# The down projections of a two-layer decoder trunk: two matmuls in place of three per weight block

## The chip, the cores and the metric

The kernel runs on one core of a Trainium2 chip. The metric is the device time of one execution in microseconds (us). Five engines work side by side, each through a queue of its own in order: TensorE multiplies (PE in the profile; PEld is its loading of weights), VectorE (DVE) and ScalarE (ACT) do elementwise work, GpSimd (POOL) does a little of it too, and SyncE (SP) issues transfers. TensorE writes its products into PSUM, which has eight banks of 512 float32 columns on 128 partitions.

## The reference, cut to what matters

The trunk has two layers, 256 tokens and a width of 1024. Layer 0 has a recurrent mixer, layer 1 sparse attention; after each comes a squared-ReLU MLP with 4096 hidden units. The part that the change touches is the second product of the MLP:

```
def _sq_relu_mlp(h, w_up, w_down):
    u = jax.nn.relu(h @ w_up)
    return (u * u) @ w_down
...
        h = _rmsnorm(x, norm_ffn[i])
        x = x + _sq_relu_mlp(h, mlp_w_up[i], mlp_w_down[i])
    return _rmsnorm(x, norm_final)
```

Everything is float32. `w_down` is 4096 by 1024 for each layer.

## The kernel before, in words

Everything is kept transposed: features on the 128 partitions, the 256 tokens along the free dimension. The residual stream `xt` is eight chunks of 128 features by 256 tokens.

To come near float32 with TensorE's rounded float32 format (`fp32r`), each operand is held as two parts, a rounded one (`h`) and the rest (`l`). A product of two operands is then three matmuls, which `mm3` (lines 373 to 377) issues for every 128 by 128 block of weights: rounded weights times rounded activations (line 375), rounded weights times the rest of the activations (line 376), and the rest of the weights times rounded activations (line 377). All three add into the same 256 columns of a bank, and each has its own load of 128 by 128 weights. The fourth product, rest times rest, is left out. The 256 tokens are read in the order 0, 128, 1, 129 and so on (`turn`), so that neighbouring columns of the bank hold tokens 128 apart (`pairs`); whoever reads the bank puts them back (`nat`).

Weights come from memory in pieces of 128 by 1024 (512 KB), in one fixed order. SP loads a piece into one of five `raw` tiles, ACT rounds it into one of seven `hi` tiles (line 322), and DVE subtracts to make one of seven `lo` tiles (line 331). In the MLPs this is driven by `tick` (line 344), called once for each piece that TensorE takes: it issues the subtraction for one piece, whatever was put off, and the rounding of the next, as long as fewer than six pieces (`LOOK`) are ahead of the one taken. The first layer's mixer and the attention have their order of work worked out by a planner beforehand (`Section`); the MLPs between them are written in program order, and each engine works through its own part of that order.

`mlp` (line 827) has two stages. The up stage makes 32 chunks of hidden units, 24 matmuls each; DVE and ACT square them and leave both parts of a chunk side by side in one tile, `uhl[i]`, rounded part in the first 256 columns, the rest in the other 256. The down stage has eight columns of output (`m`), of 32 blocks each: four pieces of weights, eight blocks to a piece, 96 matmuls in all. A column has one bank to itself, out of a ring of six. At its end DVE adds the bank to the residual (`residual`, line 589), and `epilogue(m)` starts the next norm: ACT scales the chunk, POOL squares it and adds it to a running sum. After the MLP of layer 0 this is `to_mix` (line 870), which also has DVE make the rest of the scaled chunk one `tick` later; after that of layer 1 it is `to_final` (line 1378), and there the column `m = 7` has a little more work between its third and fourth piece: four one-column matmuls (`late`, line 582) that sum the squares of the first seven chunks.

```
            for m in range(8):
                z = next(zrot)[:, :S]
...
                    wh, wl = get("dn%d" % layer, m * 4 + j)
                    for k in range(8):
                        w, i = slice(k * P, (k + 1) * P), j * 8 + k
                        mm3(z, wh[:, w], wl[:, w], uh[i], ul[i], i == 0, i == NF - 1)
                    if j == 3:
                        residual(z, m)
                        epilogue(m)
                    tick()
```

Of the kernel before, what the change touches and what calls it, by code (L numbers as in the profile page):

```python
# [12 lines left out]
F32 = mybir.dt.float32  # L13
F32R = mybir.dt.float32r
AF = mybir.ActivationFunctionType
OP = mybir.AluOpType
# [3 lines left out]
P = 128  # L20
S = 256
D = 1024
KC = D // P
NF = 32
# [248 lines left out]
def trunk_kernel(ctx: ExitStack, tc: tile.TileContext, x_in, vec_in, const_in, w2_in, wts, out):  # L273
    nc = tc.nc
    ctx.enter_context(tc.manual_schedule())
    pe, dve, act, pool = nc.tensor, nc.vector, nc.scalar, nc.gpsimd
# [9 lines left out]
    def bank(i):  # L286
        return psum.tile([P, 512], F32, name="bank%d" % i, tag="bank%d" % i)

    def rotation(*ids):
        while True:  # L290
            for i in ids:
                yield bank(i)
# [43 lines left out]
    def later(fn):  # L336
        deferred.append(fn)

    def flush():
        todo, deferred[:] = deferred[:], []  # L340
        for fn in todo:
            fn()

    def tick(lo=None, hi=None, n=1):
        for i in range(max(n, 1)):
            more = n and state["split"] - state["get"] < LOOK
            if more:
                split_lo(lo)
            if i == 0:
                flush()  # L350
            if more:
                split_hi(hi)

    def get(name, idx):
        i = state["get"]
        assert order[i] == (name, idx), (order[i], name, idx)
        state["get"] += 1
        assert state["lo"] > i
        return hi_t[i % NSPL], lo_t[i % NSPL]

    def turn(x):
        return x.rearrange("p (a b) -> p b a", a=2)

    def pairs(z):
        return z.rearrange("p (b a) -> p b a", a=2)

    def nat(z):
        return z.rearrange("p (b a) -> p a b", a=2)

    def two(x):  # L370
        return x.rearrange("p (a b) -> p a b", a=2)

    def mm3(ps, wh, wl, xh, xl, start, stop):
        ps, xh, xl = pairs(ps), turn(xh), turn(xl)
        pe.matmul(ps, wh, xh, start=start, stop=False)  # L375
        pe.matmul(ps, wh, xl, start=False, stop=False)  # L376
        pe.matmul(ps, wl, xh, start=False, stop=stop)  # L377

    def diff(o, a, h):
        return lambda e: e.tensor_tensor(o, a, h.bitcast(F32), op=OP.subtract)  # L380
# [10 lines left out]
    class Section:  # L391
# [86 lines left out]
        def proj(self, name, idx, b, t, step, xs=None, xk=None):  # L478
            wh, wl, wk = self.weight(name, idx, t)
            z = self.bank((name, idx), b, zcols)  # L480
            xs, xk = xs or [(hh[:, k], hl[:, k]) for k in range(KC)], xk or hkey
            for i in range(4):
                def run(e, i=i):
                    for k in (2 * i, 2 * i + 1):
                        w = slice(k * P, (k + 1) * P)
                        mm3(z(), wh[:, w], wl[:, w], xs[k][0], xs[k][1], k == 0, k == KC - 1)
                self.add("pe", 0.7 if self.carried else 0.68, run, r=wk + list(xk[2 * i:2 * i + 2]), w=[("ps", b)], t=t + i * step)
            return z, ("ps", b)
# [49 lines left out]
    xt = xpool.tile([P, KC, S], F32, name="xt")  # L538
# [50 lines left out]
    def residual(z, m):  # L589
        dve.tensor_tensor(two(xt[:, m]), two(xt[:, m]), nat(z), op=OP.add)  # L590


    with ExitStack() as ph:
# [41 lines left out]
        for k in range(KC):  # L635
# [6 lines left out]
                w=[("hh", k)], t=t)  # L642
# [3 lines left out]
        for q in range(4):  # L646
            for i in range(NFINE):
                w = slice(256 * q, 256 * q + 256)
# [6 lines left out]
        for a, b, n in ((0, 2, 2), (0, 1, 1), (4, 6, 2), (4, 5, 1), (0, 4, 1)):  # L655
            add("dve", 0.07 + 0.267 * n, lambda e, a=a, b=b, n=n: e.tensor_tensor(
                x2[:, a:a + n], x2[:, a:a + n], x2[:, b:b + n], op=OP.add), r=[("x2", b + i) for i in range(n)],
                w=[("x2", a + i) for i in range(n)], t=4 + a / 4)
# [44 lines left out]
        def nextbank():  # L703
            zb["n"] += 1
            return (0, 1, 2, 3, 4, 5, 7)[(zb["n"] - 1) % 7]

        def conv(m, t):
            b = nextbank()
            if m < NFINE:
                wh, wl, _ = sec.weight("in", 8 + m, t)  # L710
                z, zk = sec.bank(("in", 8 + m), b, zcols), ("ps", b)
                for k in range(KC):
                    def run(e, k=k):
                        w = slice(k * P, (k + 1) * P)
                        mm3(z(), wh[:, w], wl[:, w], hh[:, k], hl[:, k], k == 0, k == KC - 1)
                    add("pe", 0.323, run, r=[("hi0", m, k // 2), ("lo0", m, k // 2), ("hi", m), ("lo", m), hkey[k]],
                        w=[zk], t=m * 0.33 + k * NI * PJ / 2 if m < NI else t + k * PJ / 2)
            else:
                z, zk = sec.proj("in", 8 + m, b, t, PJ)
            t += 4 * PJ  # L720
            x, xk = xps[m % 3], ("xp", m % 3)
            bk = ("xb", m)
            add("dve", 0.34, lambda e: e.tensor_tensor(two(x[:, 3:]), nat(z()), two(rs), op=OP.mult), r=[zk, "rs"], w=[xk], t=t)
            add("act", 0.49, lambda e: e.activation(xb[m], x[:, 3:], AF.Identity, bias=col(V_CB, m), scale=cw(3, m)),
                r=[xk], w=[bk], t=t)
            for i in range(3):
                add("dve", 0.4, lambda e, i=i: e.scalar_tensor_tensor(xb[m], x[:, i:i + S], cw(i, m), xb[m], op0=OP.mult,
                                                                      op1=OP.add), r=[xk], w=[bk], t=t)
# [82 lines left out]
        for m in range(8):  # L811
            wh, wl, wk = sec.weight("out", m, to + 2.65 * m)
            b = nextbank()
            z = sec.bank(("out", m), b, zcols)
# [12 lines left out]
    def mlp(layer, epilogue, first, late=None):  # L827
        with ExitStack() as ph:
            up = ph.enter_context(tc.tile_pool(name="up%d" % layer, bufs=1, side="right"))
            tmp = ph.enter_context(tc.tile_pool(name="mtmp%d" % layer, bufs=2))  # L830
            uhl = [up.tile([P, 2 * S], F32R, name="uhl", tag="uhl", bufs=NF) for _ in range(NF)]
            uh, ul = [x[:, :S] for x in uhl], [x[:, S:] for x in uhl]
            zrot = rotation(*((LEADS[layer] + i) % 6 for i in range(6)))

            def up_post(m, z):
                t = tmp.tile([P, S], F32, name="t", tag="t")
                dve.scalar_tensor_tensor(two(t), nat(z), 0.0, two(rs), op0=OP.max, op1=OP.mult)  # L837
                flush()
                if m >= len(first) - 1:
                    tick(n=2 if m < 16 else 1)  # L840
                u = tmp.tile([P, S], F32, name="u", tag="u")
                act.activation(u, t, AF.Square)  # L842
                act.activation(uh[m], t, AF.Square)
                later(lambda: dve.tensor_tensor(ul[m], u, uh[m].bitcast(F32), op=OP.subtract))

            for m in range(NF):
                if m >= len(first):
                    z = next(zrot)[:, :S]
                    wh, wl = get("up%d" % layer, m)
                    for k in range(KC):  # L850
                        w = slice(k * P, (k + 1) * P)
                        mm3(z, wh[:, w], wl[:, w], hh[:, k], hl[:, k], k == 0, k == KC - 1)
                else:
                    z = first[m]()
                up_post(m, z)
            for m in range(8):
                z = next(zrot)[:, :S]
                for j in range(4):
                    if j == 3 and late and m == 7:
                        late()  # L860
                    wh, wl = get("dn%d" % layer, m * 4 + j)
                    for k in range(8):
                        w, i = slice(k * P, (k + 1) * P), j * 8 + k
                        mm3(z, wh[:, w], wl[:, w], uh[i], ul[i], i == 0, i == NF - 1)
                    if j == 3:
                        residual(z, m)
                        epilogue(m)
                    tick()

# [3 lines left out]

    nc.gpsimd.dma_start(w2raw, w2_in)
    mlp(0, to_mix, up0)


    with ExitStack() as ph:
# [108 lines left out]
        for i in range(2):  # L987
            pecol = (V_PEK, V_PEV)[i]
            add("pool", 0.15, lambda e, i=i, c=pecol: e.tensor_copy(zf[:, ZW * i + 60], vec[:, c:c + 16]), r=zok + ["vec"],
                w=[("z", i, "p")], t=-5)  # L990
# [390 lines left out]

    st = bank(6)
    mlp(1, to_final, up1, lambda: square_sums(st, acc, True, False))
    square_sums(st, sqs[1], False, True)
    act.activation(rcol, st[:, :2], AF.Sqrt, bias=epst, scale=1.0 / D)
# [120 lines left out]
```

## Time and profile before

| | us |
|---|---|
| median of three runs | 572.73 (572.32 to 572.86) |
| the profiled execution's own time | 572.76 |
| span of the profile, first to last instruction | 571.0 |
| PE busy / weight load busy in the span | 556.3 / 546.3 |
| DVE / ACT / POOL busy | 423.5 / 365.1 / 51.3 |
| down stage of layer 0 | from about 173 to 259 |
| down stage of layer 1 | from about 476 to 562 |

In the lines of the profile, L12 is line 12 of the kernel before. A group's row names the line, the engine, the operation, output and input by the program's names, shapes, and how many there are; then the busy time, the mean of one in ns, and the idle time of the engine just before them with what ended it. A row of the view in order of time has the start in us, the length in us, the engine, the line and the operation; equal neighbours are merged into one row with a count. The length of a matmul runs from its first read to a modelled end, so lengths of neighbours overlap; what one costs is the distance from its start to the next one's.

### The profile page before, as it was taken

Reading aid. Unit: us, or ns where it says so; the run is one execution under the profiler, and the core shown is the slowest. Engines: PE = TensorE matmul, PEld = TensorE weight load, DVE = VectorE, ACT = ScalarE, POOL = GpSimd, SP = SyncE. Lnnn points to the kernel's source line nnn. Section 1 sums busy time; section 2 is a strip of 40 time slices with the busy share of each in tenths; the row PEclk is TensorE's granted clock in tenths of the full one; section 3 lists DMA queues with packets and bytes.
Section 4 is the critical chain, followed back from the end, with each engine's and each line's share of the span. In section 5 each row is a group of like instructions: output and inputs, shape, how many; then the busy total and the mean of one; then the engine's idle time right before and its main releaser. Section 6 shows DMA issues by size and latency. Waiting matters only on the chain.

```text
span 571.0 us, 12231 instructions
## 1 busy us (share of the span) xinstructions
PE 556.3 (97%) x4766; PEld 546.3 (96%) x4766; DVE 423.5 (74%) x870; ACT 365.1 (64%) x724; POOL 51.3 (9%) x63
## 2 busy tenths in 40 slices
PE   8999999999999999999999999998999999999994
PEld 8999999999999999999998997988999999999994
DVE  6999999767765655657999999998867666464522
ACT  6699776756654433436898899995956654443410
POOL 0210000000000212212000101000000000232320
PEclk9999999999999999999999999999999999999998
DMA  8935465656556565566644563542766567466302
GB/s 280 404 126 196 150 225 201 225 187 206 198 189 220 185 212 194 185 203 222 218 148 162 113 198 95 137 110 95 263 202 203 202 188 247 156 204 221 130 1 73
DMA packets 32617, 105.29 MB, mean 184 GB/s; under 512 B 3984, under 2 KB 6944, under 8 KB 32560
## 3 DMA queue, kind: packets, MB, share of 16 engines
q1 hardware_dynamic: 30784, 99.70, 52.3%
q0 software_dynamic: 1200, 4.29, 3.2%
q8 instruction: 37, 0.61, 0.4%
q10 hardware_dynamic: 576, 0.53, 0.3%
q14 instruction: 20, 0.16, 0.1%
HBM read 101.36 MB, written 1.05 MB: 179 GB/s over the span
## 4 chain that ended last, share of the span: by engine, by line
PE 78%; DVE 10%; ACT 7%; issue 2%; DMA 1%; SPq 0%; DVEq 0%; ACTq 0%
PE bank L375 24%; PE bank L377 24%; PE bank L376 24%; PE bank L747 2%; ACT pt L1220 2%; DVE whl L380 2%; DVE pt L1217 1%; ACT pt L1239 1%; ACT whl L383 1%; DVE ptl L1254 1%; DMA raw<-in_dram 1%; ACT zwoh L383 1%; ACT pth L1253 1%; ACT osum L1286 1%; PE bank L1080 1%
## 5 line engine op out<-in xcount | busy, mean ns | idle before, releaser
L375 PE MATMUL bank<-hhl,whl 128*128 128x256 f32 x768 | 213.7, 278 | 0.0
L376 PE MATMUL bank<-hhl,whl 128*128 128x256 f32 x768 | 211.5, 275 | 0.8 <-DVE hhl L640 0.6
L377 PE MATMUL bank<-hhl,whl 128*128 128x256 f32 x768 | 211.3, 275 | 0.0
L376 PEld LDWEIGHTS bank<-hhl,whl 128*128 128x128 f32 x768 | 147.0, 191 | 1.4 <-DVE hhl L640 1.2
L331 DVE TENSOR_TENSOR whl<-raw,whl 128x1024 fp32r<-128x1024 f32 x117 | 146.0, 1269 | 2.8 <-ACT whl L322 2.8
L375 PEld LDWEIGHTS bank<-hhl,whl 128*128 128x128 f32 x768 | 147.0, 191 | 0.6 <-issue 0.2
L377 PEld LDWEIGHTS bank<-hhl,whl 128*128 128x128 f32 x768 | 147.1, 191 | 0.2 <-DVE whl L380 0.2
L375 PE MATMUL bank<-uhl,whl 128*128 128x256 f32 x512 | 140.9, 275 | 0.0
L376 PE MATMUL bank<-uhl,whl 128*128 128x256 f32 x512 | 140.8, 275 | 0.0
L377 PE MATMUL bank<-uhl,whl 128*128 128x256 f32 x512 | 140.8, 275 | 0.0
L322 ACT CAST whl<-raw 128x1024 fp32r<-128x1024 f32 (+1 forms) x118 | 119.7, 1038 | 22.2 <-issue 17.8
L375 PEld LDWEIGHTS bank<-uhl,whl 128*128 128x128 f32 x512 | 98.0, 192 | 0.0
L376 PEld LDWEIGHTS bank<-uhl,whl 128*128 128x128 f32 x512 | 98.0, 192 | 0.0
L377 PEld LDWEIGHTS bank<-uhl,whl 128*128 128x128 f32 x512 | 98.0, 192 | 0.0
L590 DVE TENSOR_TENSOR xt<-xt,bank 128x256 f32<-128x256 f32 x40 | 16.1, 416 | 81.8 <-PE bank L377 81.7
L380 DVE TENSOR_TENSOR whl<-raw,whl 128x1024 fp32r<-128x1024 f32 (+3 forms) x69 | 72.7, 1073 | 0.6 <-ACT whl L383 0.4
L383 ACT CAST whl<-raw 128x1024 fp32r<-128x1024 f32 (+2 forms) x64 | 60.1, 959 | 5.5 <-DMA raw<-in_dram 3.7
L842 ACT ACTIVATE u<-t 128x256 f32<-128x256 f32 x64 | 26.7, 417 | 54.0 <-DVE t L837 52.7
L837 DVE SCALAR_TENSOR_TENSOR t<-bank,rstd 128x256 f32<-128x256 f32 x64 | 26.9, 424 | 41.6 <-PE bank L377 40.7
L1380 ACT ACTIVATE xg<-xt,vec 128x256 f32<-128x256 f32 x8 | 4.1, 508 | 47.1 <-DVE xt L590 47.1
L1220 ACT ACTIVATE pt<-pt,mx 128x128 f32<-128x128 f32 (+1 forms) x64 | 28.5, 448 | 2.1 <-DVE mx L1217 2.1
L566 ACT ACTIVATE hhl<-xt,vec 128x256 fp32r<-128x256 f32 x8 | 4.1, 510 | 38.8 <-DVE xt L590 38.8
(208 smaller groups left out, 814.2 us busy)
## 6 DMA issues: line engine op xcount, KB each, us to landing
raw<-in_dram SPq DMA_DIRECT2D x171, 512.0 KB, 4.3
whl<-in_dram POOLq DMA_DIRECT2D x8, 512.0 KB, 6.2
gw<-in_dram SPq DMA_DIRECT2D x4, 512.0 KB, 8.2
raw<-in_dram SPq DMA_DIRECT2D x5, 256.0 KB, 6.0
xt<-in_dram SPq DMA_DIRECT2D x4, 256.0 KB, 5.1
zwol<-in_dram SPq DMA_DIRECT2D x2, 512.0 KB, 5.4
raw<-in_dram SPq DMA_DIRECT2D x2, 456.0 KB, 3.9
kh<-th SPq DMA_DIRECT2D x8, 64.0 KB, 3.7
```

The lines of the kernel that those rows point to most:

```text
L322: (act.copy if eng is None else eng.tensor_copy)(hi_t[i % NSPL][:, :n], raw_t[i % NRAW][:, :n])
L331: (eng or dve).tensor_tensor(lo[:, :n], raw_t[i % NRAW][:, :n], hi[:, :n].bitcast(F32), op=OP.subtract)
L375: pe.matmul(ps, wh, xh, start=start, stop=False)
L376: pe.matmul(ps, wh, xl, start=False, stop=False)
L377: pe.matmul(ps, wl, xh, start=False, stop=stop)
L380: return lambda e: e.tensor_tensor(o, a, h.bitcast(F32), op=OP.subtract)
L383: return lambda e: (e.copy if e is act else e.tensor_copy)(o, a)
L590: dve.tensor_tensor(two(xt[:, m]), two(xt[:, m]), nat(z), op=OP.add)
L747: e.matmul(z(), gw[b][:, o:o + P], xb[2 * b + k], start=k == 0, stop=k == 1)
L837: dve.scalar_tensor_tensor(two(t), nat(z), 0.0, two(rs), op0=OP.max, op1=OP.mult)
L842: act.activation(u, t, AF.Square)
L1220: add("act", (0.39, 0.49)[qc], lambda e, row=row, j=j: e.activation(row, row, AF.Exp, bias=mx[:, j:j + 1], scale=-1.0, accum_out=sm[:, j:j ...
```

## The change

For the columns `m = 0` to `6` of both layers' down stages, the two products that have the rounded weights become one matmul: its moving operand is the whole of `uhl[i]`, 512 columns, rounded part first and then the rest, each with tokens alternating as before. It fills the whole bank: the first half gets rounded weights times rounded activations, the second half rounded weights times the rest. The third product adds into the first half as before. At the end of such a column ACT copies the second half of the bank into a new tile `part`, DVE adds the first half to the residual as before, and a second DVE instruction adds `part`. The column `m = 7` keeps `mm3`. The tile `part` (128 by 256, float32, one buffer) is new in the MLP's pool. Weights, transfers and everything else stay as they are.

```
+    def mm2(z, wh, wl, x, start, stop):
+        xd = x.rearrange("p (i a b) -> p i b a", i=2, a=2)
+        pe.matmul(z.rearrange("p (i b a) -> p i b a", i=2, a=2), wh, xd, start=start, stop=False)
+        pe.matmul(pairs(z[:, :S]), wl, xd[:, 0], start=False, stop=stop)
...
+            part = [tmp.tile([P, S], F32, name="part", tag="part", bufs=1)]
...
             for m in range(8):
-                z = next(zrot)[:, :S]
+                z = next(zrot)
...
-                        mm3(z, wh[:, w], wl[:, w], uh[i], ul[i], i == 0, i == NF - 1)
+                        if m < 7:
+                            mm2(z, wh[:, w], wl[:, w], uhl[i], i == 0, i == NF - 1)
+                        else:
+                            mm3(z[:, :S], wh[:, w], wl[:, w], uh[i], ul[i], i == 0, i == NF - 1)
                     if j == 3:
-                        residual(z, m)
+                        if m < 7:
+                            act.copy(two(part[0]), nat(z[:, S:]))
+                        residual(z[:, :S], m)
+                        if m < 7:
+                            dve.tensor_tensor(xt[:, m], xt[:, m], part[0], op=OP.add)
                         epilogue(m)
                     tick()
```

## The prediction

> **What bounds the kernel now.** I read the page first, then the groups by line, then the view in order of time at the places that resemble the new instructions. The page:
>
> ```profile
> span 571.0 us, 12231 instructions
> ...
> PE 556.3 (97%) x4766; PEld 546.3 (96%) x4766; DVE 423.5 (74%) x870; ACT 365.1 (64%) x724; POOL 51.3 (9%) x63
> ...
> PEclk9999999999999999999999999999999999999998
> ```
>
> TensorE hardly ever stands still and its clock is granted in full, so only the rate at which it starts matmuls counts. The page's means of a matmul's length don't give that rate. It comes from the first and last start of one line over many blocks; here line 377, the last of each triple, in six columns of layer 1's down stage (window 486 to 550 us):
>
> ```profile
> L377 PE MATMUL bank<-uhl,whl x192: 275/275/275, 486.0 to 550.0; 128*128 128x256 f32 x192
> ```
>
> Each lasts 275 ns, yet 191 triples go by in 64.0 us: 335.1 ns a triple, 111.7 ns a matmul. No engine and no transfer holds this stream up, so what sets 111.7 ns is the question. Two limits are near: the moving columns, and the load of weights that goes with each matmul. Narrow matmuls show the load alone (lengths are merged over 16 and 15 instructions):
>
> ```profile
> 301.80 1.95 PE L1016 MATMUL bank<-zwoh,zwol 128*128 128x122 f32 x16
> 301.92 1.75 PEld L1016 LDWEIGHTS bank<-zwoh,zwol 128*128 128x128 f32 x15
> ```
>
> The L1016 matmul has 122 columns, less than half. With 0.275 us for the last one, as line 377 shows for its own, 15 steps take 1.95 - 0.275 = 1.675 us: some 111.7 ns each, the same as with 256 columns. That is the floor of one load per matmul. Wider ones show the columns alone:
>
> ```profile
> 272.37 0.29 PE L1080 MATMUL bank<-whl,hhl 128*128 128x304 f32 x1
> ...
> 273.92 0.29 PE L1080 MATMUL bank<-whl,hhl 128*128 128x304 f32 x1
> ```
>
> The twelve steps between (1.55 us) take 129.2 ns each with 304 columns, above the floor. So today's 256 columns wait for their load, by little, and three loads a block are the price.
>
> **The change part by part.** (1) Per block, two matmuls of 256 columns and their loads of the same weights go, and one of 512 with one load comes. The old down stage has none of that width; the attention's scores do, with the same alternating order, rounded operands and accumulation. There two of 512 are followed by one of 256:
>
> ```profile
> 288.52 0.38 PE L1210 MATMUL bank<-kh,sb 128*128 128x512 f32 x1
> 288.73 0.38 PE L1211 MATMUL bank<-kl,sb 128*128 128x512 f32 x1
> 288.95 0.27 PE L375 MATMUL bank<-hhl,whl 128*128 128x256 f32 x1
> 289.06 0.28 PE L376 MATMUL bank<-hhl,whl 128*128 128x256 f32 x1
> ...
> 324.24 0.38 PE L1210 MATMUL bank<-kh,sb 128*128 128x512 f32 x1
> ...
> 324.79 0.28 PE L376 MATMUL bank<-hhl,whl 128*128 128x256 f32 x1
> ...
> 336.51 0.38 PE L1210 MATMUL bank<-kh,sa 128*128 128x512 f32 x1
> ...
> 337.05 0.28 PE L1211 MATMUL bank<-kl,sa 128*128 128x256 f32 x1
> ```
>
> From the first start of 512 to the start after the 256: 0.54, 0.55 and 0.54 us, mean 543.3 ns. Taking off one load floor (111.7) leaves 215.8 ns for each 512. It fits the line through the 304 columns: (215.8 - 129.2) / 208 = 0.416 ns a column, which puts 256 columns at 109.2 ns, 2.5 under the floor.
>
> In the new stream 512 and 256 take turns. The load for the 256 hides under the 512 (111.7 in 215.8). The load for the next 512 starts when the 256 starts and needs 111.7, more than its columns. So a pair takes 215.8 + 111.7 = 327.5 ns where the triple takes 335.1: 7.6 ns less. There are 2 layers x 7 columns x 32 blocks = 448 pairs: 448 x 7.6 = 3.4 us off the path of TensorE.
>
> Bounds of this price: the two 512 and the 256 lie between 0.54 and 0.55 us in rows rounded to 0.01, so a 512 lies between about 214 and 219 ns ((0.54 or 0.55 - 0.1117) / 2), or 220 with the rounding. At 220 a pair takes 331.7 and the gain is 1.5 us. On the other side, if two loads fit into the room of one pair, the 256 goes at its columns' 109.2, the pair takes 325.0 and the gain is 10.1 x 448 = 4.5 us. I take 7.6, the middle of the rows.
>
> (2) At the end of each of the 14 columns ACT gets a copy out of the bank, DVE an addition. Rows of their kind, an ACT copy of 128x256 from a bank and a DVE product of two 128x256 operands in the same memory:
>
> ```profile
> L503 ACT COPY rstd<-bank 128x256 f32<-128x256 f32 x4 | 1.5, 371 | 6.5 <-PE bank L587 6.5
> ```
>
> ```profile
> 562.67 0.42 DVE L555 TENSOR_TENSOR sq<-xt 128x256 f32<-128x256 f32 x1
> ```
>
> So 0.37 + 0.42 us a column, 14 x 0.79 = 11.1 us if nothing hid them. What hides them is seen between two columns of layer 0, on DVE and on ACT:
>
> ```profile
> 195.06 0.42 DVE L590 TENSOR_TENSOR xt<-xt,bank 128x256 f32<-128x256 f32 x1 [5.00 <-PE bank L377]
> 195.40 1.22 DVE L331 TENSOR_TENSOR whl<-raw,whl 128x1024 fp32r<-128x1024 f32 x1
> ...
> 205.78 0.42 DVE L590 TENSOR_TENSOR xt<-xt,bank 128x256 f32<-128x256 f32 x1 [4.46 <-PE bank L377]
> ```
>
> ```profile
> 206.23 0.51 ACT L566 ACTIVATE hhl<-xt,vec 128x256 fp32r<-128x256 f32 x1 [4.83 <-DVE xt L590]
> ```
>
> DVE stands 4.46 us and ACT 4.83 us of each column's 10.72 before the next one ends. ACT's copy waits for TensorE at the point where ACT today waits for DVE; queued behind it are the chunk's scaling (L566) and the next roundings (L322). The copy runs beside DVE's residual, then the addition follows; if the two reads of the bank are ordered, the chain from the column's end to L331 grows by 0.37 + 0.42, at most some 0.9 us. Who waits is TensorE, for the `lo` tile that L331 writes at 195.40 to 196.62. By `tick` that tile is for the fifth piece after the one just taken, four pieces of eight triples later: 195.0 + 4 x 2.68 = 205.7. It has 9 us in hand, so the 0.9 cost nothing. Without that cover part 2 would turn the forecast into a loss of 7.7 us.
>
> The bank of a column is wanted again six columns later, some 63 us, so its longer emptying holds nobody. POOL gets its chunk 0.4 to 0.9 us later. In layer 1 the sum of squares must be ready for the matmuls within the last column:
>
> ```profile
> 552.17 0.73 POOL L562 TENSOR_TENSOR acc<-acc,sq 128x256 f32<-128x256 f32 x1
> ...
> 558.82 0.50 PE L582 MATMUL bank<-ones,acc 128*128 128x1 f32 x4
> ```
>
> It is there at 552.9 and wanted at 558.8: 5.9 us to spare. `m = 7` is untouched, so the tail behind the last matmul is too. SP, POOL's queue and the transfers get nothing new, but TensorE takes weights 2.3% faster (7.6 of 335.1). In the second half of layer 1's down stage, columns: PE, PEld, DVE, ACT, POOL busy, clock, share of the transfer engines, GB/s:
>
> ```profile
> 500.00:530.00 30.00, 30.00 (x271) 30.00 (x270) 15.02 (x15) 11.03 (x14) 7.43 (x5) 1.00 0.63 210
> ```
>
> At a share of 0.63 they follow.
>
> (3) The sum: 572.76 (own time of the profiled execution; its span of 571.0 and the 1.8 us around it both stay but for the 3.4) - 3.4 = 569.4. The median lies 0.03 lower, so 569.3 us, 0.6% less, half of it in each layer.
>
> **The rivals.** *A: the 512 pays for its breadth (slower).* The attention's other matmuls of that width are dearer:
>
> ```profile
> 315.51 0.40 PE L1277 MATMUL bank<-pth,vhl 128*128 128x512 f32 x1
> ...
> 315.99 0.28 PE L1275 MATMUL bank<-pth,vhl 128*128 128x256 f32 x1
> ...
> 316.23 0.27 PE L1210 MATMUL bank<-kh,sa 128*128 128x256 f32 x1
> ```
>
> Two of 512 take 0.48 us and two of 256 0.24: 240 and 120 ns, a pair 360, which is 24.9 over the triple: +11.2 us, 583.9. If only the 512 pays, 240 + 111.7 is 16.6 over: +7.4 us, 580.2. For it: the new operand's halves are a second pattern that no row has exactly. Against: L1277 reads runs of 256 neighbouring columns, the new one alternates like L1210. It decides from 223.4 ns for a 512 (335.1 - 111.7). I give it 7%, at 580.
>
> *B: both loads hide,* 325.0 a pair, 568.2 us. For: the room is there, 325.0 against two loads of 223.4. Against: loads start one by one, each with its matmul (L1016's loads step like its matmuls). 10%.
>
> *C: the excess over the columns stays with the block.* Today's triple is 335.1 against 3 x 109.2 = 327.6 of columns. If its 7.5 ns belong to something that comes once a block, a pair takes 325.0 + 7.5 = 332.5, and the gain is 2.6 x 448 = 1.2 us: 571.6. Against: L1016 shows the floor at each matmul. 5%.
>
> The Trainium skill, page "TensorE: Matmul & The Clock Gate", section "Back-to-back issue gap", speaks against most of the gain: by its formula for the isolated gap (columns at 2.4 per ns plus 2.5 ns) 512 columns take 215.8 ns and 256 take 109.2, so that the joining saves only one 2.5 ns a block, 1.1 us in all. The trace agrees with it on 512, but not on a stream of 256 with a load each, which it shows at 111.7.
>
> *D: the gain is taken back:* the down stage ends earlier and then waits for weights in flight, or the attention does at its start. 572.7 us, no change. Against: the share of 0.63 and no idle time of TensorE in the down stage. 6%.
>
> *E: the end of a column holds TensorE (slower):* the copy, L590 and the addition in a row, with L322 and L331 queued behind them. Deciding once the chain grows by 9 us, when at worst all 11.1 us of part 2 would show: 572.7 - 3.4 + 11.1 = 580.4. The growth worked out is a tenth of that. 3%.
>
> **How the numbers follow.** Forecast 69% (its own range 568.5 to 571.2, from the bounds of the 512), B 10%, D 6%, A 7%, C 5%, E 3%. The range from 567.9 to 571.9 holds the forecast, B and C, 84%. A measurement of this kernel can tell about 0.2%, 1.15 us, from no change, so the border is 571.6: the forecast, B and half of C lie under it, with a little taken off the forecast's upper end: faster 0.80. D, the other half of C and that end: same 0.10. A and E: slower 0.10.
>
> **What would show it.** The 512 of the new line should start 216 to 218 ns before its partner, and the partner 109 to 112 before the next; the third product's line, over 192 blocks, should span 191 x 0.3275 = 62.6 us in place of 64.0, and the residuals (L590) of one layer lie 10.48 us apart in place of 10.72. TensorE should show 448 matmuls and loads fewer, 4318, ACT 14 more and DVE 14 more, with the idle time before L590 still near 4 us. A 512 at 223 or more makes A true; a pair at 325 B, at 332 C. Idle time of PEld before an `hhl` or `uhl` matmul, released by L331, or by a transfer, would make E or D true and my part 2 wrong.

## The result, and the profile after

The changed kernel takes 569.62 us, median of six runs (569.40 to 570.25); the kernel before took 572.83 beside it (572.32 to 573.34). The ratio is 0.9945, 95% interval 0.9932 to 0.9958: 3.2 us faster. The profiled execution took 569.74 us, its span is 567.9 where it was 571.0.

The page of the changed kernel. Its lines 381 and 382 are the two matmuls of `mm2`, 595 is the residual, 876 the copy on ACT, 879 the addition of `part`:

```profile
span 567.9 us, 11331 instructions
...
PE 553.5 (97%) x4318; PEld 531.4 (94%) x4318; DVE 429.3 (76%) x884; ACT 370.2 (65%) x738; POOL 51.1 (9%) x63
...
PEclk9999999999999999999999999999999999999997
...
L381 PE MATMUL bank<-uhl,whl 128*128 128x512 f32 x448 | 146.8, 382 | 0.0
...
L382 PE MATMUL bank<-uhl,whl 128*128 128x256 f32 x448 | 122.1, 273 | 0.0
```

There are 448 matmuls and loads fewer, and 14 instructions more on ACT and on DVE each. TensorE is busy for the same 97% of a shorter span, so the page alone can't say what a pair costs: 382 ns and 273 ns are lengths, and neighbours overlap. The view in order of time has the distances (start in us, length, engine, line, operation):

```profile
199.92 0.27 PE L382 MATMUL bank<-uhl,whl 128*128 128x256 f32 x1
200.03 0.38 PE L381 MATMUL bank<-uhl,whl 128*128 128x512 f32 x1
200.25 0.27 PE L382 MATMUL bank<-uhl,whl 128*128 128x256 f32 x1
200.36 0.38 PE L381 MATMUL bank<-uhl,whl 128*128 128x512 f32 x1
200.58 0.27 PE L382 MATMUL bank<-uhl,whl 128*128 128x256 f32 x1
```

From one 512 to the next it is 0.33 us. Sharper is the row that gives the first and last start of line 382, the last matmul of each pair, over the seven columns of layer 0's down stage, 224 pairs:

```profile
L382 PE MATMUL bank<-uhl,whl x224: 272/273/273, 174.0 to 247.1; 128*128 128x256 f32 x112
```

That is 73.1 us over 223 steps, 327.8 ns with the rounding of 0.1 us, for 335.1 ns a triple before. Nothing between the columns breaks the stream. Between two columns of layer 0, DVE first and then ACT:

```profile
195.45 0.42 DVE L595 TENSOR_TENSOR xt<-xt,bank 128x256 f32<-128x256 f32 x1 [4.36 <-ACT part L876]
195.91 0.42 DVE L879 TENSOR_TENSOR xt<-xt,part 128x256 f32<-128x256 f32 x1
196.25 1.22 DVE L331 TENSOR_TENSOR whl<-raw,whl 128x1024 fp32r<-128x1024 f32 x1
...
205.93 0.42 DVE L595 TENSOR_TENSOR xt<-xt,bank 128x256 f32<-128x256 f32 x1 [3.76 <-ACT part L876]
```

```profile
195.05 0.37 ACT L876 COPY part<-bank 128x256 f32<-128x256 f32 x1 [4.31 <-PE bank L382]
196.36 0.51 ACT L571 ACTIVATE hhl<-xt,vec 128x256 fp32r<-128x256 f32 x1 [0.95 <-DVE xt L879]
...
205.53 0.37 ACT L876 COPY part<-bank 128x256 f32<-128x256 f32 x1 [4.31 <-PE bank L382]
```

The residual waits for ACT's copy, not for TensorE: the two reads of the bank are put in order. L331 starts 1.20 us after the first instruction that waited for the column's end (195.05 to 196.25), where it was 0.34 before (195.06 to 195.40), so the chain grew by 0.86 us. DVE is still idle for 3.76 us and ACT for 4.31 before the next end, and the residuals lie 10.48 us apart in place of 10.72.

### The profile page after: what moved, and what is told of

It reads as the page before. It is cut to its first block, busy times and chain, and to the rows that moved or that the text cites. A ratio compares the mean times of both kernels' runs of the same rounds, so it can differ in the third digit from the quotient of the medians.

```text
span 567.9 us, 11331 instructions
## 1 busy us (share of the span) xinstructions
PE 553.5 (97%) x4318; PEld 531.4 (94%) x4318; DVE 429.3 (76%) x884; ACT 370.2 (65%) x738; POOL 51.1 (9%) x63
## 4 chain that ended last, share of the span: by engine, by line
PE 77%; ACT 10%; DVE 8%; issue 2%; DMA 1%; SPq 1%; DVEq 0%; ACTq 0%
PE bank L381 17%; PE bank L375 15%; PE bank L376 15%; PE bank L377 15%; PE bank L382 9%; PE bank L752 2%; ACT pt L1233 2%; ACT pt L1252 2%; ACT whl L388 2%; ACT pth L1266 1%; DMA raw<-in_dram 1%; DVE whl L385 1%; DVE pt L1230 1%; ACT zwoh L388 1%; ACT osum L1299 1%
## 5 line engine op out<-in xcount | busy, mean ns | idle before, releaser
L331 DVE TENSOR_TENSOR whl<-raw,whl 128x1024 fp32r<-128x1024 f32 x117 | 146.0, 1269 | 2.8 <-ACT whl L322 2.8
L381 PE MATMUL bank<-uhl,whl 128*128 128x512 f32 x448 | 146.8, 382 | 0.0
L382 PE MATMUL bank<-uhl,whl 128*128 128x256 f32 x448 | 122.1, 273 | 0.0
L381 PEld LDWEIGHTS bank<-uhl,whl 128*128 128x128 f32 x448 | 84.7, 189 | 11.8
L382 PEld LDWEIGHTS bank<-uhl,whl 128*128 128x128 f32 x448 | 86.0, 192 | 0.0
L876 ACT COPY part<-bank 128x256 f32<-128x256 f32 x14 | 5.2, 372 | 61.8 <-PE bank L382 61.8
L850 DVE TENSOR_TENSOR uhl<-u,uhl 128x256 fp32r<-128x256 f32 x64 | 26.6, 416 | 1.8 <-ACT uhl L849 1.7
L565 POOL TENSOR_TENSOR acc<-xt 128x256 f32<-128x256 f32 x2 | 2.9, 1460 | 265.3 <-issue 152.4
L565 POOL TENSOR_TENSOR sq<-xt 128x256 f32<-128x256 f32 x12 | 17.3, 1442 | 94.6 <-DVE xt L879 86.5
```

What stands on the lines that cost most here:

```text
L331: (eng or dve).tensor_tensor(lo[:, :n], raw_t[i % NRAW][:, :n], hi[:, :n].bitcast(F32), op=OP.subtract)
L381: pe.matmul(z.rearrange("p (i b a) -> p i b a", i=2, a=2), wh, xd, start=start, stop=False)
L382: pe.matmul(pairs(z[:, :S]), wl, xd[:, 0], start=False, stop=stop)
```

## The experiments

Four kernels ran beside each other first, then four more. In both sets the kernel before was timed too (572.90 us and 573.06 us).

**The work between columns alone.** Three matmuls a block again, but the bank is emptied in two halves as in the changed kernel.

```
     def mm2(z, wh, wl, x, start, stop):
         xd = x.rearrange("p (i a b) -> p i b a", i=2, a=2)
-        pe.matmul(z.rearrange("p (i b a) -> p i b a", i=2, a=2), wh, xd, start=start, stop=False)
+        for h in range(2):
+            pe.matmul(pairs(z[:, h * S:(h + 1) * S]), wh, xd[:, h], start=start and h == 0, stop=False)
         pe.matmul(pairs(z[:, :S]), wl, xd[:, 0], start=False, stop=stop)
```

> The work between columns alone: three matmuls a block as in the kernel before (the rest of the activations goes to the bank's second half as a matmul of its own), with the changed kernel's copy on ACT and addition on DVE at the end of the 14 columns. My theory (the gain is all in the 448 pairs, the emptying is hidden): triples of 335.1 ns again and 572.8 us, the time before, within 0.5. Rival E (the end of a column holds TensorE): above it, up to 572.8 + 14 x 0.79 = 583.9 us.

Measured: 572.94 us, ratio to the kernel before 0.9998 (0.9989 to 1.0007). The third product's row (line 383 here) over layer 0's seven columns:

```profile
L383 PE MATMUL bank<-uhl,whl x224: 275/275/275, 173.8 to 248.5; 128*128 128x256 f32 x112
```

74.7 us over 223 steps are 335.0 ns a triple, as before the change. The emptying alone costs and gains nothing that can be measured, so rival E falls.

**The joined matmuls alone.** The bank's second half is computed and never read: in columns 0 to 6 the product of the rounded weights and the rest of the activations is left out of the sum.

```
                     if j == 3:
-                        if m < 7:
-                            act.copy(two(part[0]), nat(z[:, S:]))
                         residual(z[:, :S], m)
-                        if m < 7:
-                            dve.tensor_tensor(xt[:, m], xt[:, m], part[0], op=OP.add)
                         epilogue(m)
```

> The joined matmuls alone: as the changed kernel, but the bank's second half is never read, so the product of rounded weights and the rest of the activations is left out of columns 0 to 6. My theory: 569.6 us as the changed kernel, within 0.5, since the copy and the addition lie in the idle time of ACT and DVE. Rival E: lower than 569.6 by what the emptying costs.

Measured: 569.75 us, ratio 0.9942 (0.9929 to 0.9954). The changed kernel's ratio, 0.9945, lies within this interval. So, as far as the intervals tell, the whole gain is in the pairs, and none of it is eaten between the columns.

**The floor of a load.** The third product takes half of its columns.

```
-        pe.matmul(pairs(z[:, :S]), wl, xd[:, 0], start=False, stop=stop)
+        pe.matmul(pairs(z[:, :S])[:, :64], wl, xd[:, 0, :64], start=False, stop=stop)
```

> The floor of a load: as the changed kernel, but the third product (rest of the weights) takes 128 of the 256 columns, so half of it is left out. My theory (beside a 512 the second matmul costs the load of the next weights, 111.7 ns, and not its own columns): the pair stays at 327.5 ns and the time at 569.6 us, within 0.5. Rival C (columns cost, and an excess stays with the block): 128 columns less are 53 ns a pair, 448 x 53 = 24 us less, 546 us.

Measured: 569.66 us, ratio 0.9940 (0.9927 to 0.9954). Half the columns of that matmul are gone and the time stays. Matmuls and loads in order of time, then the row over layer 0's seven columns:

```profile
199.81 0.22 PE L382 MATMUL bank<-uhl,whl 128*128 128x128 f32 x1
199.81 0.19 PEld L381 LDWEIGHTS bank<-uhl,whl 128*128 128x128 f32 x1
199.86 0.43 PE L381 MATMUL bank<-uhl,whl 128*128 128x512 f32 x1
199.92 0.19 PEld L382 LDWEIGHTS bank<-uhl,whl 128*128 128x128 f32 x1
200.13 0.22 PE L382 MATMUL bank<-uhl,whl 128*128 128x128 f32 x1
200.14 0.19 PEld L381 LDWEIGHTS bank<-uhl,whl 128*128 128x128 f32 x1
200.19 0.43 PE L381 MATMUL bank<-uhl,whl 128*128 128x512 f32 x1
200.25 0.19 PEld L382 LDWEIGHTS bank<-uhl,whl 128*128 128x128 f32 x1
200.46 0.22 PE L382 MATMUL bank<-uhl,whl 128*128 128x128 f32 x1
```

```profile
L382 PE MATMUL bank<-uhl,whl x224: 219/219/219, 173.6 to 246.6; 128*128 128x128 f32 x112
```

73.0 us over 223 steps are 327.4 ns a pair. What the narrow matmul gives up, 0.06 in place of 0.11 us to the next start, the 512 behind it takes: 0.27 in place of 0.22, and its recorded length grows from 0.38 to 0.43. The loads do not move closer: the load for the 512 starts with the narrow matmul (200.14), and the next load follows 0.11 us later (200.25). The floor is thus kept between loads, not between the starts of matmuls. From that next load to the next narrow matmul it is 0.21 us, about what a 512 costs. Read so, the 512's recorded start comes before its weights are in, and only the sum over a pair is a price. This settles rival C, by which some 546 us were expected: the pair's excess over its columns is the floor of a load, not something that comes once a block.

**Rival A's price.** The pairs read their columns in natural order, so that the bank holds the tokens in that order, and it is emptied in that order.

```
     def mm2(z, wh, wl, x, start, stop):
-        xd = x.rearrange("p (i a b) -> p i b a", i=2, a=2)
-        pe.matmul(z.rearrange("p (i b a) -> p i b a", i=2, a=2), wh, xd, start=start, stop=False)
-        pe.matmul(pairs(z[:, :S]), wl, xd[:, 0], start=False, stop=stop)
+        pe.matmul(z, wh, x, start=start, stop=False)
+        pe.matmul(z[:, :S], wl, x[:, :S], start=False, stop=stop)
...
-                            act.copy(two(part[0]), nat(z[:, S:]))
-                        residual(z[:, :S], m)
+                            act.copy(part[0], z[:, S:])
+                            dve.tensor_tensor(xt[:, m], xt[:, m], z[:, :S], op=OP.add)
+                        else:
+                            residual(z[:, :S], m)
```

> Rival A's price: as the changed kernel, but the pairs read their 512 and 256 columns in natural order, neighbours one after the other, and the bank is emptied in that order. By the rows of L1277 and L1275 a 512 takes 235 to 240 ns and the 256 after it 112 to 120, a pair 347 to 360 in place of 327.5: 8.7 to 14.6 us more, 578 to 584 us. If the order of columns does not matter here: 569.6 us.

Measured: 581.13 us, ratio 1.0145 (1.0131 to 1.0158): 11.5 us more than the changed kernel.

```profile
L382 PE MATMUL bank<-uhl,whl x224: 278/279/284, 175.0 to 253.8; 128*128 128x256 f32 x112
```

78.8 us over 223 steps are 353.4 ns a pair, 18 more than a triple in alternating order. So rival A had the right price for the other order: pairs in natural order lose against triples in alternating order. No run has triples in natural order, so what the joining is worth in that order alone is not shown, nor why the order counts.

**The column that was left out.** `m = 7` takes the pairs too.

```
-                        if m < 7:
+                        if m < 8:
...
-                        if m < 7:
+                        if m < 8:
...
-                        if m < 7:
+                        if m < 8:
```

> The column that was left out: m = 7 takes the joined matmuls and the emptying too. My theory: 64 more pairs save 64 x 7.6 = 0.5 us, but behind the last column nothing hides the emptying, so each layer's tail grows by the copy and the addition, 0.37 + 0.42 us and the hand-over, 1.6 to 1.8 us for both: 570.7 to 570.9 us in place of 569.6. If the emptying were free there too: 569.1 us.

Measured: 571.21 us, ratio 0.9966 (0.9954 to 0.9979): faster than before, but some 1.3 us slower than the changed kernel's ratio would give beside it (573.06 x 0.9945 = 569.9). That is the upper end of what was expected (570.9 - 569.6). Behind the last matmul of layer 1:

```profile
559.31 0.37 ACT L876 COPY part<-bank 128x256 f32<-128x256 f32 x1 [9.10 <-PE bank L382]
559.72 0.42 DVE L595 TENSOR_TENSOR xt<-xt,bank 128x256 f32<-128x256 f32 x1 [10.04 <-ACT part L876]
560.17 0.43 DVE L879 TENSOR_TENSOR xt<-xt,part 128x256 f32<-128x256 f32 x1
560.63 0.51 ACT L1393 ACTIVATE xg<-xt,vec 128x256 f32<-128x256 f32 x1 [0.95 <-DVE xt L879]
561.18 0.61 PE L587 MATMUL bank<-ones,sq 128*128 128x1 f32 x4 [1.96 <-DVE sq L560]
```

In the changed kernel, TensorE's row at that place:

```profile
560.23 0.60 PE L587 MATMUL bank<-ones,sq 128*128 128x1 f32 x4 [1.04 <-DVE sq L560]
```

TensorE waits 1.96 us for the squares instead of 1.04. The same copy and addition that cost nothing between columns cost 0.9 us at the end of layer 1. Behind layer 0 it is about the same: from the last start of its down stage to the first of layer 1's, the trace of this kernel has 217.8 us (257.0 to 474.8) and that of the changed kernel 216.7 (257.8 to 474.5).

**How much cover there is.** Nine, then 18 additions on DVE into a tile that nobody reads, behind the addition of `part`, at each of the 14 columns.

```
+            pad = tmp.tile([P, S], F32, name="pad", tag="pad", bufs=1)
...
                             dve.tensor_tensor(xt[:, m], xt[:, m], part[0], op=OP.add)
+                            for _ in range(9):
+                                dve.tensor_tensor(pad, part[0], part[0], op=OP.add)
```

> How much cover there is: as the changed kernel, with 9 additions of 128x256 into an unused tile on DVE behind the addition of part, at each of the 14 columns. They take about 9 x 0.34 = 3.1 us, less than DVE's idle 3.76 us a column and than the 9 us in hand of TensorE. My theory: 569.6 us, within 0.5. Rival E (TensorE is held by the end of a column): 569.6 + 14 x 3.1 = up to 613 us.

> The same with 18 additions, 6.1 us a column: 2.4 us more than DVE's idle time. My theory: DVE then sets the pace of a column, 10.48 + 2.4 us; over seven columns of a layer it falls 16 us behind, of which the 9 us in hand take off a part: 5 to 10 us late in each layer, 580 to 590 us. If less is in hand than I think: up to 569.6 + 2 x 16 = 602 us; if TensorE depends on DVE less: 570 us.

Measured: 570.10 us with nine (ratio 0.9947, 0.9934 to 0.9961), 621.58 with 18 (ratio 1.0843, 1.0826 to 1.0859). The first time came as expected, with a load of 4.4 us a column in place of the 3.1 worked out. The second did not: it is above even the worst case given. DVE between two columns, with nine and with 18:

```profile
184.67 0.42 DVE L595 TENSOR_TENSOR xt<-xt,bank 128x256 f32<-128x256 f32 x1 [5.25 <-ACT part L877]
185.13 0.43 DVE L880 TENSOR_TENSOR xt<-xt,part 128x256 f32<-128x256 f32 x1
185.47 4.39 DVE L882 TENSOR_TENSOR pad<-part 128x256 f32<-128x256 f32 x9
...
195.19 0.42 DVE L595 TENSOR_TENSOR xt<-xt,bank 128x256 f32<-128x256 f32 x1 [0.39 <-ACT part L877]
```

```profile
199.43 0.41 DVE L595 TENSOR_TENSOR xt<-xt,bank 128x256 f32<-128x256 f32 x1
199.88 0.42 DVE L880 TENSOR_TENSOR xt<-xt,part 128x256 f32<-128x256 f32 x1
200.22 8.94 DVE L882 TENSOR_TENSOR pad<-part 128x256 f32<-128x256 f32 x18
209.08 1.22 DVE L331 TENSOR_TENSOR whl<-raw,whl 128x1024 fp32r<-128x1024 f32 x1
...
214.02 0.42 DVE L595 TENSOR_TENSOR xt<-xt,bank 128x256 f32<-128x256 f32 x1
```

The size of the load was off: from the first of the 18 to the start of L331 it is 8.86 us, 0.49 each and not 0.34. DVE then has no idle time left before the residual, and its column takes 14.59 us (199.43 to 214.02) in place of 10.48: 4.1 us over, where 2.4 were expected. The row of the pairs in layer 0's seven columns:

```profile
L382 PE MATMUL bank<-uhl,whl x224: 272/273/580, 174.4 to 264.4; 128*128 128x256 f32 x112
```

They take 90.0 us, 16.9 more than in the changed kernel (73.1). From the first residual of the layer to the seventh DVE takes 87.1 us (185.25 to 272.39) where the changed kernel has 62.9 (184.91 to 247.85): 24.2 us of delay on DVE. So some 7 us of it were taken up by the tiles in hand, near the 8 us that are left of the prediction's 9 when the chain has grown by 0.86. What holds TensorE is the subtraction that makes the `lo` tile, as the view of waits says of both layers (us in all, times, longest):

```profile
PE bank L382 <- DVE whl L331: 20.7, 10, 3.8
```

The granted clock was 0.94 from 185 to 265 us, where the changed kernel has 1.00 from 174 to 247; how much of the 16.9 us this makes is not shown. Of the 52.8 us by which the span grew (567.9 to 620.7), 43.4 lie in the two down stages with their eighth columns (106.6 us in place of 84.0, and 105.2 in place of 84.4), and 8.7 between them; what these 8.7 come from is not shown.

With nine, 4.4 us of added work a column fill DVE's idle time almost wholly (0.39 us are left), and TensorE loses nothing that can be told.

**The same joining in the up projections.** From the first column that the planner doesn't issue, 29 in layer 0 and 28 in layer 1.

```
-            def up_post(m, z):
+            def up_post(m, z, wide=False):
                 t = tmp.tile([P, S], F32, name="t", tag="t")
-                dve.scalar_tensor_tensor(two(t), nat(z), 0.0, two(rs), op0=OP.max, op1=OP.mult)
+                if wide:
+                    act.copy(two(part[0]), nat(z[:, S:]))
+                    dve.tensor_tensor(two(t), two(part[0]), nat(z[:, :S]), op=OP.add)
+                    dve.scalar_tensor_tensor(t, t, 0.0, rs, op0=OP.max, op1=OP.mult)
+                else:
+                    dve.scalar_tensor_tensor(two(t), nat(z), 0.0, two(rs), op0=OP.max, op1=OP.mult)
...
-                        mm3(z, wh[:, w], wl[:, w], hh[:, k], hl[:, k], k == 0, k == KC - 1)
+                        if wide:
+                            mm2(z, wh[:, w], wl[:, w], hhl[:, k].rearrange("p i s -> p (i s)"), k == 0, k == KC - 1)
+                        else:
+                            mm3(z[:, :S], wh[:, w], wl[:, w], hh[:, k], hl[:, k], k == 0, k == KC - 1)
```

> The same joining in the up projections, from the first column that the planner does not issue: 29 columns in layer 0 and 28 in layer 1, 8 blocks each, 456 pairs; at the end of each, ACT copies the bank's second half, DVE adds it to the first, and the relu and the norm follow from there. My theory: 456 x 7.6 = 3.5 us less than the changed kernel, 566.1 us, if DVE (about 1.8 + 0.34 of 2.62 us a column) and ACT (1.7 + 0.33) keep up. Rival: the longer chain between columns holds TensorE, because ACT's copy waits in order ahead of the rounding of weights: 0.3 us and more a column, 57 x 0.3 = 17 us, 583 us or more.

Measured: 567.03 us, ratio 0.9895 (0.9881 to 0.9909), below the changed kernel's interval: it beats both kernels, by 6.0 us the one before. The pairs of layer 0's up stage (line 383 here is the second of a pair), and the busy time of the engines from 100 to 170 us (PE, PEld, DVE, ACT, POOL, clock, share of the transfer engines, GB/s) in this kernel and then in the changed one:

```profile
L383 PE MATMUL bank<-hhl,whl x232: 272/273/273, 97.0 to 172.6; 128*128 128x256 f32 x116
```

```profile
100.00:170.00 70.00, 70.00 (x430) 64.33 (x429) 62.22 (x112) 56.58 (x114) 0.00 (x0) 1.00 0.62 206
```

```profile
100.00:170.00 70.00, 70.00 (x629) 70.00 (x628) 49.95 (x82) 45.52 (x84) 0.00 (x0) 1.00 0.59 201
```

75.6 us over 231 steps are 327.3 ns a pair in the up stage too. DVE goes from 49.95 to 62.22 of 70 us, so there is little left. The gain over the changed kernel is about 2.9 us by the ratios (573.06 x (0.9945 - 0.9895)). The pairs are as forecast, and the intervals, some 0.8 us to each side, do not tell 2.9 from the 3.5 expected.

## Why the prediction was right

Forecast 569.3 us, measured 569.62.

1. *A triple is three load floors, 335.1 ns.* Shown for the pair by the half third product: 128 columns less in 448 matmuls changed nothing, and the loads kept their 0.11 us. What bounds a pair beside its 512 is the load of the next weights. For the triple it rests on the narrow rows of L1016; no run changed the triple's columns.
2. *A pair takes 327.5 ns.* The 512 was priced at 215.8 from six matmuls of the attention. The down stage of the changed kernel has 327.8 ns by its row, the run with half a third product 327.4, both from starts rounded to 0.1 us. 448 x 7.5 = 3.4 us; the median fell by 3.2. By the interval of the ratio the gain is 2.4 to 3.9 us, which leaves out the 4.5 of rival B and the 1.2 of rival C. The single distances came as forecast, 0.22 and 0.11 us in the rows. That a 512 could start so long before its partner that it shows 0.27, as it does behind the narrow matmul, I had not thought of; it doesn't change the sum.
3. *The emptying costs nothing.* Shown from both sides: with it alone 572.94 beside 572.90, without it 569.75 beside the changed kernel's 569.62. The prediction first had the copy run beside the residual, and that did not hold; the case it allowed for, "the two reads of the bank are ordered", is what came, and the chain grew by 0.86 us of the 0.9 allowed. The price without cover, 0.79 us a column, was seen in the kernel with all eight columns: 0.9 us of waiting at the end of layer 1.
4. *Nothing is taken back.* Idle time before the residual in the down stages is still near 4 us (4.36 and 3.76), the clock stays at full, and of 3.4 us worked out 3.2 arrive, so rival D falls.

Of the rivals, A's price was measured for the natural order (353.4 ns, where 347 to 360 were expected from L1277 and L1275) and does not hold for the alternating one. B would have shown 325.0 ns a pair and C 332.5; the rows of 327.4 and 327.8 exclude both with their 0.5 ns of rounding. The formula for the isolated gap in the section "Back-to-back issue gap" of the Trainium skill's page "TensorE: Matmul & The Clock Gate", by which 1.1 us would have been gained, gave the right 512 and the wrong 256. The section offers it for a matmul by itself and says that with loads in the stream both set the spacing, which is what the rows show. With a load for each matmul a step is 111.7 ns at 256 and at 122 columns, and a pair of 512 and 128 columns takes 327.4 ns, which leaves 111.6 beside the 215.8 of the 512.

## What to carry to other kernels

Where each matmul has its own load of weights, look whether the distance between starts still falls when the columns get fewer. If it doesn't, as here, the load is the bound. Two products with the same weights are then better one matmul with twice the columns, on two conditions. The wide matmul must cost less than two floors: here 215.8 ns against 223.4, while in natural order its rows show 0.23 to 0.24 us and the time rose. And the extra emptying must lie where the emptying engines stand idle, not at the end of a stage. Price such a change from the sum over a repeating group of matmuls, because single start distances shift between neighbours.

## What was not expected of the hardware

A 512-column matmul was recorded 0.27 us before its successor when the matmul ahead of it was narrow, and 0.22 when that was 256 wide, at the same 327 ns a pair: the recorded start is not always the start of the columns. And 18 additions in a row into one tile took 0.49 us each. In the changed kernel the next instruction starts 0.34 us after the addition of `part` where it works on another tile (195.91 to 196.25), and 0.46 after the residual where it reads what that wrote (195.45 to 195.91). What makes the difference was not tested.
